# A transpose on one core: TensorE's program as a loop with decrementing semaphores, and the load issued ahead of the pending store

## Chip, cores, metric

One Trainium2 chip, one of its cores. The metric is the device time of the core in microseconds (us), the median of several executions. Input and output are 256 MB each in HBM, the memory outside the core.

## The reference

```python
def setup_inputs():
    return {"x": np.random.randn(8192, 8192).astype(np.float32)}

def reference(x):
    return np.transpose(x)
```

## The kernel before

The matrix is handled in 128 *row chunks*, in two *slabs* (column halves) of 64. A chunk is 128 rows by 4096 columns, 2 MB. It is loaded into one of three buffers in SBUF, the core's own memory. TensorE transposes it in 32 blocks of 128 x 128, four blocks to a bank of PSUM (the memory that TensorE writes), eight banks. ScalarE copies the even banks and VectorE the odd ones into *regions*; a region collects one group of four output row blocks over eight chunks (2 MB) and is then stored. Windows are staggered, so that in the steady state each chunk closes exactly one window: per chunk one 2 MB load and one 2 MB store. At the end of a slab all eight windows close at once, with 1 to 8 chunks in them (256 KB to 2 MB). All DMAs go through one queue, issued by SyncE.

```python
S, B, W = 32, 4, 8
NR, NIN, NREG, NPS = S // B, 3, 9, 8
...
for t in range(NIN):
    load(t)
n = 0
for t, (s, c) in enumerate(chunks):
    nc.tensor.wait_ge(s_ld[t % NIN], 16 * (t // NIN + 1))    # counts that only grow
    closing = []
    for q in [(c + k) % NR for k in range(NR)]:              # the order turns with the chunk
        if q not in window:
            ... r = free.pop(0); the copy engine waits until region r's last store has landed
        ps = pss[n % NPS]
        if bank[n % NPS] is not None:
            nc.tensor.wait_ge(*bank[n % NPS])
        for b in range(B):
            last = nc.tensor.transpose(ps[...], ins[t % NIN][...], ident)
        last.then_inc(s_pe, 1)
        n += 1
        (nc.scalar, nc.vector)[e].wait_ge(s_pe, n)
        cp = ... copy of the bank into the region
        cp.then_inc(s_cp[e], 1)
        copied[e] += 1
        bank[(n - 1) % NPS] = (s_cp[e], copied[e])
        if c == end:
            closing.append((q, e, copied[e]))
    for q, e, count in closing:                              # the pending store first
        nc.sync.wait_ge(s_cp[e], count)
        ... store of the region
    if t + NIN < len(chunks):                                # then the next load
        nc.sync.wait_ge(s_pe, n)
        load(t + NIN)
```

## Time and profile before

| | before |
|---|---|
| time, median of 3 | 1266.07 us (1265.91 to 1267.67) |
| DMA rate over the span | 425 GB/s; 426 to 431 in nearly all slices |
| TensorE busy | 57% |
| one row chunk (load + store) | 9.79 us in the mean |
| median 16 KB DMA packet | 611 ns, so 16 engines move 429 GB/s |

First the slices of the profiled execution (the span in 40 equal parts: busy tenths of the DMA engines, then GB/s), with the DMA queues below (packets, MB, share of the 16 engines' span):

```profile
DMA  9999999999999999999999999999999999999998
GB/s 380 418 428 427 428 429 428 427 428 428 426 428 429 426 428 430 429 428 428 428 417 428 428 427 428 431 429 429 429 428 428 430 428 430 429 429 429 428 428 353
DMA packets 39308, 537.51 MB, mean 425 GB/s; under 512 B 4320, under 2 KB 4832, under 8 KB 6240
## 3 DMA queue, kind: packets, MB, share of 16 engines
q1 hardware_dynamic: 39264, 536.89, 100.0%
q8 instruction: 32, 0.52, 0.2%
q14 instruction: 12, 0.10, 0.0%
```

The kernel is bound by its DMA engines from end to end: no slice but the first two (380 and 418), the slab change (417) and the last is more than 1% off the 429 GB/s that the packets allow. Besides the data, 32 packets of 16 KB carry instructions (q8). They come about every 39 us (the median), which is four chunks, so one per 256 of TensorE's 8192 matrix instructions; one takes 1.0 us at the median (0.94 to 1.10). I call them *fetches*. (q14 is a second queue of instruction packets, 12 of 8 KB, 309 ns each.)

Then the waits (engine and line, for whom; us in total, times, longest):

```profile
ACT reg L142 <- PE ps L131: 902.7, 501, 7.7
DVE reg L144 <- PE ps L131: 850.8, 499, 10.3
PEld ps L131 <- DMA in<-in_x_dram: 520.8, 123, 6.1
...
ACT reg L142 <- DMA out_dram<-reg: 33.8, 6, 13.5
DVE reg L144 <- DMA out_dram<-reg: 33.4, 5, 18.1
```

Everybody waits down a chain that starts at the load. The copies wait for a store only 11 times, and 65 of these 67 us are at the slab change: in the steady state a region is free just in time.

The DMA issues (KB each, median us from issue to landing):

```profile
in<-in_x_dram SPq DMA_DIRECT2D x128, 2048.0 KB, 23.5
out_dram<-reg SPq DMA_DIRECT2D x114, 2048.0 KB, 22.7
```

23.5 us is almost five transfers of 4.9 us: the queue is always deep.

One more reading needs the trace itself. The trace has 16 increments of a semaphore for each transfer, each with its own time (4320 for the 270 transfers), and the profile counts 16 DMA engines. I read them as one from each engine, when its share has landed; the pace agrees (at 16 packets of 611 ns an engine needs 9.78 us per chunk, and loads 75 to 127 landed 9.79 us apart in the mean), but the trace does not say which engine an increment belongs to. Read so, the 16 times, here sorted, show how far the engines have come apart. The times of three transfers, in us after the first of the 16:

```
load 0           0.0 .. 0.3                                                            spread 0.3
load 20          0.0 .. 2.8                                                            spread 2.8
last store       0.0 0.1 0.1 0.5 0.7 1.0 1.8 2.6 3.3 4.2 4.4 4.7 5.5 5.5 5.9 5.9       first at 1257.7 us, last at 1263.7
```

The spread grows mostly in steps: five of 1.0 to 1.6 us, each seen at a load that landed 3 to 8 us after the start of an instruction packet. The kernel waits for all 16 increments of its stores, so it ends with the slowest of the 16 engines (1263.7 us, in a span of 1265.1).

### The profile page before, as it was taken

The page shows a single profiled execution, that of the slowest core. Times are in us where ns is not written, and L with a number is a line of the kernel's source. Part 1 is how long each engine was busy: PE and PEld are TensorE (multiplying, and loading weights), DVE is VectorE, ACT ScalarE, POOL GpSimd, SP SyncE. Part 2 cuts the span into 40 slices and gives each one's busy share as a digit, 9 for nine tenths or more (in the row PEclk, how much of TensorE's full clock was granted, in tenths as well). Part 3 has the DMA queues.
Part 4 walks back from the last instruction along what each step waited for, and adds up shares of the span by engine and source line. Part 5 has one row for each costly group of instructions (what it writes and reads, how often), then busy time and mean ns, then how long its engine had stood idle before and what let it go on. Part 6 is the DMA issues. An engine that isn't in the chain of part 4 may idle for free.

```text
span 1265.1 us, 9814 instructions
## 1 busy us (share of the span) xinstructions
PE 722.6 (57%) x4096; PEld 690.6 (55%) x4096; DVE 353.5 (28%) x512; ACT 300.7 (24%) x513; POOL 0.7 (0%) x6
## 2 busy tenths in 40 slices
PE   6555656665556555565456655656566555665651
PEld 6555645555456555564455555655455555565551
DVE  3322222322223222232133322223223222232220
ACT  3322222222222222222122222222222222222220
POOL 0000000000000000000000000000000000000000
PEclk8877686777776877768667777686867877777675
DMA  9999999999999999999999999999999999999998
GB/s 380 418 428 427 428 429 428 427 428 428 426 428 429 426 428 430 429 428 428 428 417 428 428 427 428 431 429 429 429 428 428 430 428 430 429 429 429 428 428 353
DMA packets 39308, 537.51 MB, mean 425 GB/s; under 512 B 4320, under 2 KB 4832, under 8 KB 6240
## 3 DMA queue, kind: packets, MB, share of 16 engines
q1 hardware_dynamic: 39264, 536.89, 100.0%
q8 instruction: 32, 0.52, 0.2%
q14 instruction: 12, 0.10, 0.0%
HBM read 268.44 MB, written 268.44 MB: 424 GB/s over the span
## 4 chain that ended last, share of the span: by engine, by line
DMA 78%; PE 20%; issue 0%; DVE 0%; ACT 0%; SPq 0%; ACTq 0%
DMA in<-in_x_dram 75%; PE ps L131 20%; DMA out_dram<-reg 2%; DVE reg L144 0%; ACT reg L142 0%; SPq L197 0%; SPq L68 0%; ACTq L140 0%
## 5 line engine op out<-in xcount | busy, mean ns | idle before, releaser
L131 PE MATMUL ps<-ident,in 128*128 128x128 f32 x4096 | 722.6, 359 | 514.8 <-DMA in<-in_x_dram 499.7
L131 PEld LDWEIGHTS ps<-ident,in 128*128 128x128 f32 x4096 | 690.6, 193 | 546.5 <-DMA in<-in_x_dram 520.8
L144 DVE COPY reg<-ps 128x512 f32<-128x512 f32 x512 | 353.5, 692 | 884.2 <-PE ps L131 850.8
L142 ACT COPY reg<-ps 128x512 f32<-128x512 f32 x512 | 299.4, 586 | 936.5 <-PE ps L131 902.7
L142 ACT ACT_TABLE_LOAD x1 | 1.3, 1283 | 0.9 <-SPq L68 0.9
L83 POOL TENSOR_SCALAR_AFFINE_SELECT ident<-ident 128x128 f32<-128x128 f32 x1 | 0.3, 292 | 0.2 <-POOL ident L81 0.2
L81 POOL MEMSET ident<- 128x128 f32 x1 | 0.2, 204 | 0.5 <-SPq L68 0.5
L186 POOL MEMSET const-bfloat16-1.0<- 128x1 bf16 x1 | 0.1, 101 | 0.0
L186 POOL MEMSET const-uint8-127<- 128x1 uint8 x1 | 0.1, 101 | 0.0
L186 POOL MEMSET const-float32-0.0<- 128x1 f32 x1 | 0.1, 98 | 0.2 <-issue 0.2
L186 POOL MEMSET const-float32-1.0<- 128x1 f32 x1 | 0.1, 98 | 0.0
## 6 DMA issues: line engine op xcount, KB each, us to landing
in<-in_x_dram SPq DMA_DIRECT2D x128, 2048.0 KB, 23.5
out_dram<-reg SPq DMA_DIRECT2D x114, 2048.0 KB, 22.7
out_dram<-reg SPq DMA_DIRECT2D x4, 1792.0 KB, 20.1
out_dram<-reg SPq DMA_DIRECT2D x4, 1536.0 KB, 19.2
out_dram<-reg SPq DMA_DIRECT2D x4, 1280.0 KB, 19.1
out_dram<-reg SPq DMA_DIRECT2D x4, 1024.0 KB, 17.9
out_dram<-reg SPq DMA_DIRECT2D x4, 768.0 KB, 16.3
out_dram<-reg SPq DMA_DIRECT2D x4, 512.0 KB, 13.2
```

The costliest lines, as they stand in the source:

```text
L81: nc.gpsimd.memset(ident, 0.0).then_inc(s_id, 1)
L83: nc.gpsimd.affine_select(out=ident, in_=ident, compare_op=mybir.AluOpType.not_equal, fill=1.0, base=0, pattern=[[-1, P]], channel_multipl ...
L131: last = nc.tensor.transpose(ps[:, b * P:(b + 1) * P], ins[t % NIN][:, (q * B + b) * P:(q * B + b + 1) * P], ident,)
L142: cp = nc.scalar.copy(out=o, in_=i)
L144: cp = nc.vector.tensor_copy(out=o, in_=i)
L186: nc = _bacc.Bacc("TRN2", target_bir_lowering=False, num_devices=1)
```

## The change

The intent: TensorE's 8192 matrix instructions become two chunks written out and 42 turns of a loop over three chunks, so that the fetches all along the run fall away. Every turn of this loop runs the same instructions, with the same counts and the same banks: so the counts do not grow, but each semaphore is brought down when it has been waited for, and each bank has its own; and the bank order does not turn with the chunk, but is fixed. And SyncE issues the next load ahead of the pending store.

```diff
-        pss = [... for k in range(NPS)]
+        pss = [... for k in range(NR)]
+        s_bank = [nc.alloc_semaphore(f"s_bank{q}") for q in range(NR)]
+        def transposes(t):
+            k = t % NIN
+            nc.tensor.sem_inc(s_ld[k], -16).wait_op(s_ld[k], 16, "sem-ge")
+            for q in range(NR):
+                if t:
+                    nc.tensor.sem_inc(s_bank[q], -1).wait_op(s_bank[q], 1, "sem-ge")
+                for b in range(B):
+                    tr = nc.tensor.transpose(pss[q][...], ins[k][...], ident)
+                    if b == B - 1:
+                        tr.then_inc(s_pe, 1)
+        for t in range(T % NIN):
+            transposes(t)
+        with nc.Fori(0, T // NIN, engines=[nc.tensor.engine]):
+            for t in range(NIN):
+                transposes(T % NIN + t)
...
-            nc.tensor.wait_ge(s_ld[t % NIN], 16 * (t // NIN + 1))
-            for q in [(c + k) % NR for k in range(NR)]:
+            for q in range(NR):
...
-                cp.then_inc(s_cp[e], 1)
-                copied[e] += 1
-                bank[(n - 1) % NPS] = (s_cp[e], copied[e])
                 if c == end:
+                    cp.then_inc(s_cp[e], 1)
+                    copied[e] += 1
                     closing.append((q, e, copied[e]))
+                    eng.wait_ge(s_cp[e], copied[e])
+                    eng.sem_inc(s_bank[q], 1)
+                else:
+                    cp.then_inc(s_bank[q], 1)
+            if t + NIN < T:
+                nc.sync.wait_ge(s_pe, (t + 1) * NR)
+                load(t + NIN)
             for q, e, count in closing:
                 ... store
-            if t + NIN < len(chunks):
-                nc.sync.wait_ge(s_pe, n)
-                load(t + NIN)
```

More of the change, by code (lines that the diff above doesn't have):

```diff
@@ L63 @@
     NREG = 9
-    NPS = 8
     CH = N // P
@@ L72 @@
         regs = [nc.alloc_sbuf_tensor(f"reg{k}", [P, B * W * P], dt).ap() for k in range(NREG)]
-        pss = [nc.alloc_psum_tensor(f"ps{k}", [P, B * P], dt).ap() for k in range(NPS)]
+        pss = [nc.alloc_psum_tensor(f"ps{k}", [P, B * P], dt).ap() for k in range(NR)]
         s_id = nc.alloc_semaphore("s_id")
@@ L91 @@
         ).then_inc(s_id, 1)
-        nc.tensor.wait_ge(s_id, 2)
         chunks = [(s, c) for s in range(M // J) for c in range(CH)]
@@ L100, in load @@
             ).then_inc(s_ld[t % NIN], 16)
+        def transposes(t):
[5 more added lines that the diff above has]
+                for b in range(B):
+                    tr = nc.tensor.transpose(
+                        pss[q][:, b * P:(b + 1) * P],
+                        ins[k][:, (q * B + b) * P:(q * B + b + 1) * P],
+                        ident,
+                    )
+                    if b == B - 1:
+                        tr.then_inc(s_pe, 1)
+        T = len(chunks)
+        nc.tensor.wait_ge(s_id, 2)
+        for t in range(T % NIN):
[3 more added lines that the diff above has]
+                transposes(T % NIN + t)
         for t in range(NIN):
             load(t)
-        n = 0
         copied = [0, 0]
-        bank = [None] * NPS
         free = list(range(NREG))
@@ L112 @@
         for t, (s, c) in enumerate(chunks):
-            nc.tensor.wait_ge(s_ld[t % NIN], 16 * (t // NIN + 1))
             closing = []
-            for q in [(c + k) % NR for k in range(NR)]:
+            for q in range(NR):
+                e = q % 2
+                eng = (nc.scalar, nc.vector)[e]
                 if q not in window:
@@ L121 @@
                     if stored[r]:
-                        (nc.scalar, nc.vector)[q % 2].wait_ge(s_st[r], 16 * stored[r])
+                        eng.wait_ge(s_st[r], 16 * stored[r])
                 c0, end, r = window[q]
@@ L125 @@
                 view = regs[r][:, :B * rows].rearrange("p (b i) -> p b i", b=B)
-                ps = pss[n % NPS]
-                e = q % 2
-                if bank[n % NPS] is not None:
-                    nc.tensor.wait_ge(*bank[n % NPS])
-                for b in range(B):
-                    last = nc.tensor.transpose(
-                        ps[:, b * P:(b + 1) * P],
-                        ins[t % NIN][:, (q * B + b) * P:(q * B + b + 1) * P],
-                        ident,
-                    )
-                last.then_inc(s_pe, 1)
-                n += 1
                 o = view[:, :, (c - c0) * P:(c - c0 + 1) * P]
-                i = ps.rearrange("p (b i) -> p b i", b=B)
-                (nc.scalar, nc.vector)[e].wait_ge(s_pe, n)
+                i = pss[q].rearrange("p (b i) -> p b i", b=B)
+                eng.wait_ge(s_pe, t * NR + q + 1)
                 if e == 0:
```

## The prediction

> **What bounds it now.** The DMA engines. The slices show them over 90% busy, at 426 to 431 GB/s nearly everywhere; the queue table gives 537.5 MB in 1265.1 us. TensorE is busy 57%. A row chunk takes 9.87 us (two 2 MB transfers), its 32 transposes 4 to 6 us (timeline). DMA is 78% of the chain of waits. A 16 KB packet takes 611 ns at the median: 429 GB/s for 16 engines, the bytes' own limit.
>
> Not all of the span is bytes. The last slice has 353 GB/s. The 16 increments of the last store land from 1257.7 to 1263.7 us: the slowest engine ends 5.9 us after the fastest, and the kernel waits for it. This spread is 0.3 us at the start and steps up by about 1.5 us when one of the 32 instruction packets of q8 (16 KB, about 1.0 us each) falls on an engine that was not ahead. They come every 39 us, which is four chunks, 256 TensorE instructions. [...] 32 x 1.5 us over 16 engines is 3 us in the mean, about 6 us on the slowest.
>
> **What the change does.**
> 1. TensorE's 8192 instructions become two chunks plus a loop of three (about 220 instructions, 14 KB). If the loop stays resident, q8 falls from 32 packets to 2 to 5. The slowest engine then ends near the fastest's time less its own fetches: 0.5 us under 1257.7, plus 1 to 1.5 us of skew from the small q14 fetches, which stay. Gain about 5 us.
> 2. About 9 decrements per chunk on TensorE. At 51 ns each in this trace: 0.5 us per chunk, off the path.
> 3. Fixed bank order and load before store. The load is issued no earlier (it still waits for the chunk's last transpose); the store goes out about 5 us later, one queue place (4.9 us) behind. It lands some 10 us later against the loads. A region that was free just in time (store landed 322.7 us, wanted at about 323) now holds up copies until about 15 us after their chunk landed, and so TensorE's next chunk. By my recurrence the next load is still issued 13 us before its place in the queue begins, so the engines should not run dry. New waits, no time lost.
>
> **Time.** 1266.07 - 5 = about 1261 us; range 1257 to 1272. Faster by 2% would need under 1241, which 537 MB at 429 GB/s (1251 us) excludes. Faster 1%, same 95%, slower 4%.
>
> **What would show it.** q8 at 5 packets or fewer; last landings within 2 us; last slice near 390 GB/s; copies waiting for store DMAs in most chunks (over 300 us, not 67); load to landing 20, not 23.5 us.
>
> **What would make it wrong.** [...] Slower by 2% needs the queue to run dry: GB/s below 425 in every slice.

The sum came to 1266.07 - 5 = about 1261 us: 5.9 us of spread that the last stores show, less the 1 to 1.5 us for q14, plus 0.5, make the 5. The q14 figure is an estimate of mine, the 14 KB of the loop is 220 times the 64 bytes that 32 packets of 16 KB come to over 8192 instructions, and that the loop stays resident was an assumption. On a loop that fetches at every turn, with one chance in three, the prediction named 1268 to 1278 us.

## The result

| | before | changed |
|---|---|---|
| median of 4 runs | 1266.87 us (1265.91 to 1269.5) | 1269.79 us (1268.77 to 1272.34) |
| ratio | | 1.0023, 95% interval 1.0001 to 1.0045: the same, within 2% |
| span of the profiled run | 1265.1 us | 1267.8 us |

A ratio is the mean time of one kernel's fast runs over that of the other's of the same rounds, so not quite the ratio of the medians. The time lies inside the predicted range, but a gain of 5 us was predicted and it became 3 us longer.

The slices and queues of the changed kernel:

```profile
DMA  9999999999999999999999999999999999999997
GB/s 384 418 428 426 430 428 430 430 428 430 429 428 430 429 429 430 429 430 430 426 380 428 428 429 430 430 430 430 430 429 430 430 430 430 428 428 430 430 429 315
DMA packets 39277, 537.00 MB, mean 424 GB/s; under 512 B 4320, under 2 KB 4832, under 8 KB 6240
## 3 DMA queue, kind: packets, MB, share of 16 engines
q1 hardware_dynamic: 39264, 536.89, 99.8%
q14 instruction: 12, 0.10, 0.0%
q8 instruction: 1, 0.02, 0.0%
```

The instruction packets went from 32 to 1, and most slices are a little faster (430 where there was 428). But the slab change fell from 417 to 380 and the last slice from 353 to 315.

Its waits and issues:

```profile
ACT reg L154 <- DMA out_dram<-reg: 780.1, 66, 17.3
DVE reg L156 <- DMA out_dram<-reg: 770.5, 66, 23.9
PEld ps L111 <- issue: 598.0, 201, 9.3
PE ps L111 <- PEq L109: 541.9, 187, 9.1
```

```profile
in<-in_x_dram SPq DMA_DIRECT2D x128, 2048.0 KB, 19.6
out_dram<-reg SPq DMA_DIRECT2D x114, 2048.0 KB, 24.4
```

The copies now wait for stores about once per chunk (132 times), 1551 us in all, as predicted, and the loads sit shorter in the queue. TensorE's waits stand under its sequencer (PEq) now; the trace has 1147 semaphore instructions on TensorE, 51 ns each, where the kernel before has 131. None of this starves the engines in the steady state: 430 GB/s.

Where the time went is seen in the landings. I split each run at four transfers, and give the slowest and the mean of the 16 engines. In the changed kernel the load stands one place (4.89 us, eight packets of 611 ns) earlier in the queue than before, so 4.89 is added to its first stretch and taken from its last:

| us | to load 60 | loads 60 to 75 (slab change) | loads 75 to 127 | to the end | sum |
|---|---|---|---|---|---|
| slowest, before | 573.9 | 148.3 | 509.2 | 32.2 | 1263.7 |
| slowest, changed | 573.5 | 149.7 | 511.0 | 32.3 | 1266.5 |
| mean, before | 571.4 | 148.0 | 509.0 | 32.2 | 1260.6 |
| mean, changed | 569.6 | 150.6 | 507.9 | 33.9 | 1262.1 |

The mean engine gains 1.8 us in the first slab and 1.1 us in the second, the 3 us of fetches that were predicted. It gives back 2.6 us at the slab change and 1.7 us at the end. And the slowest engine, which sets the time, gains almost nothing in the first slab (0.4 us) and *loses* 1.4 us at the slab change and 1.7 us (before rounding) in the second slab: these make the 2.8 us. At the last load the 16 increments stand like this (us after the first):

```
before    0.0 0.1 0.1 0.5 0.6 1.0 1.9 2.6 3.2 4.2 4.4 4.7 5.4 5.5 5.9 5.9
changed   0.0 0.0 0.1 0.1 0.2 0.5 0.5 0.9 1.2 1.3 1.3 1.4 1.7 2.2 4.4 7.4
```

Before, with the fetches, the engines are spread over 5.9 us, none more than 1.0 us behind the next. Now fourteen engines lie within 2.2 us, and one is 7.4 us behind. In the second slab its lag over the first engine grows by 68 ns per chunk (the median over loads 75 to 126), nearly every chunk. Before, this median is 0: there the lag mainly jumps, by 1.35 and 1.46 us, at loads that landed at 677 and 987 us, 4 and 7 us after the start of a fetch. I call this steady growth the *drift*. With it comes a set of 16 KB packets of 625 to 640 ns, slightly too long, which fall mostly in times when TensorE transposes (83% of them at their middle, against 56% of all 16 KB packets): 196 in the changed kernel, 40 in the one before (between 80 and 1200 us, without 600 to 700). That they run on the engine that falls behind is not shown; their time over 611 ns sums to 3.9 us (0.8 before), less than that engine's lag.

### The profile page after: what moved, and what is told of

The parts are those of the page before. It is cut to its first block, busy times and chain, and to the rows that moved or that the text cites. A ratio compares the mean times of both kernels' runs of the same rounds, so it can differ in the third digit from the quotient of the medians.

```text
span 1267.8 us, 11057 instructions
## 1 busy us (share of the span) xinstructions
PE 685.6 (54%) x4096; PEld 637.6 (50%) x4096; DVE 330.2 (26%) x512; ACT 278.2 (22%) x513; POOL 0.7 (0%) x6
## 5 line engine op out<-in xcount | busy, mean ns | idle before, releaser
L111 PE MATMUL ps<-ident,in 128*128 128x128 f32 x4096 | 685.6, 342 | 551.0 <-PEq L109 541.9
L111 PEld LDWEIGHTS ps<-ident,in 128*128 128x128 f32 x4096 | 637.6, 182 | 598.8 <-issue 598.0
L156 DVE COPY reg<-ps 128x512 f32<-128x512 f32 x512 | 330.2, 686 | 908.5 <-DMA out_dram<-reg 770.5
L154 ACT COPY reg<-ps 128x512 f32<-128x512 f32 x512 | 276.9, 597 | 960.7 <-DMA out_dram<-reg 780.1
## 6 DMA issues: line engine op xcount, KB each, us to landing
in<-in_x_dram SPq DMA_DIRECT2D x128, 2048.0 KB, 19.6
out_dram<-reg SPq DMA_DIRECT2D x4, 1536.0 KB, 19.6
out_dram<-reg SPq DMA_DIRECT2D x4, 512.0 KB, 15.1
```

Source lines behind the costliest of these rows:

```text
L111: tr = nc.tensor.transpose(pss[q][:, b * P:(b + 1) * P], ins[k][:, (q * B + b) * P:(q * B + b + 1) * P], ident,)
L154: cp = nc.scalar.copy(out=o, in_=i)
L156: cp = nc.vector.tensor_copy(out=o, in_=i)
```

## The experiments

Eighteen runs, each beside runs of the kernel before on the same chip. "Drift" and "packets" are as just defined, from the one profile of each run. "Last load" is the lag of the last engine there.

| run | median us | ratio, 95% interval | q8 packets | drift, ns per chunk | packets | last load, us |
|---|---|---|---|---|---|---|
| before | 1266.87 | | 32 | 0 | 40 | 5.9 |
| changed | 1269.79 | 1.0023 (1.0001 to 1.0045) | 1 | 68 | 196 | 7.4 |
| e1_unrolled | 1267.82 | 1.0005 (0.9988 to 1.0021) | 36 | 44 | 243 | 5.5 |
| e2_store_first | 1268.7 | 1.0012 (0.9986 to 1.0039) | 1 | 101 | 440 | 10.5 |
| e3_big_first | 1269.23 | 1.0016 (1.0000 to 1.0031) | 1 | 66 | 207 | 6.2 |
| e4_before_load_first | 1268.53 | 1.0006 (0.9990 to 1.0022) | 32 | 1 | 74 | 6.1 |
| e5_before_fixed_order | 1267.22 | 1.0002 (0.9986 to 1.0017) | 32 | 8 | 40 | 5.8 |
| e6_before_decrements | 1267.78 | 1.0000 (0.9985 to 1.0016) | 36 | 93 | 399 | 9.0 |
| e7_more_semaphores | 1274.45 | 1.0056 (1.0040 to 1.0072) | 1 | 103 | 222 | 10.1 |
| e8_few_semaphores | 1270.33 | 1.0026 (1.0011 to 1.0041) | 1 | 59 | 194 | 6.4 |
| e9_decrement_loads | 1266.0 | 0.9991 (0.9974 to 1.0008) | 32 | 1 | 36 | 6.3 |
| e10_decrement_banks | 1268.56 | 1.0022 (0.9995 to 1.0048) | 35 | 0 | 32 | 6.2 |
| e11_idle_semaphores | 1271.91 | 1.0041 (1.0019 to 1.0062) | 36 | 0 | 86 | 6.2 |
| e12_closing_step | 1266.39 | 0.9992 (0.9974 to 1.0010) | 32 | 0 | 35 | 6.3 |
| c1_changed_again | 1269.69 (one) | | 1 | 66 | 189 | 9.3 |
| c2_decrements_again | 1270.67 (one) | | 36 | 96 | 433 | 9.5 |
| c3_banks_again | 1268.7 (one) | | 35 | 2 | 60 | 6.3 |
| c4_idle_sems_again | 1267.57 (one) | | 36 | 0 | 155 | 6.2 |
| f1_loads_on_act | 1268.2 | 1.0003 (0.9985 to 1.0020) | 1 | 80 | 182 | 9.5 |
| f2_loads_on_act_orders | 1273.43 | 1.0031 (1.0005 to 1.0058) | 1 | 101 | 480 | 10.6 |

The kernel before, run beside them, itself scatters from 1265.2 to 1271.5 us, with 11 of its 40 runs in the timed batches above 1269. So a difference of 1 or 2 us in time is not settled by six runs; the landings in the profiles tell more than the times, but each is of one run.

The drift is a median: it tells whether the lag grows steadily, not by how much. It parts the kernels clearly in the second slab: with it the lag grows by over 20 ns in 61 to 100% of the chunks, without it in 8 to 20%. In the mean the growth is 66 ns per chunk in the changed kernel and 33 in the one before, but 57 in e1 (drift) and 58 in c4 (none). In the first slab (loads 10 to 60) the median is 0 to 102 ns in the kernels with drift and -16 to 0 in the others; an engine that falls behind shows in this measure only once it is the last.

### e1: without the loop

```diff
-        for t in range(T % NIN):
+        for t in range(T):
             transposes(t)
-        with nc.Fori(0, T // NIN, engines=[nc.tensor.engine]):
-            for t in range(NIN):
-                transposes(T % NIN + t)
```

> The changed kernel with TensorE's loop written out, decrements and order kept. Theory F (the loop saves the instruction fetches): q8 rises from 1 packet to 32 or more, each costs one engine 1.5 us, so about 3 us per engine in the mean and 1 to 3 us in time: 1271 to 1273 us, ratio to the kernel before 1.003 to 1.005. Rival L (the loop itself costs, by a slow drift of one DMA engine, 60 ns per chunk, that the kernel before does not show): the last engine no longer drifts, and the time is 1266 to 1269 us.

Measured: 1267.8 us. The queues of this kernel:

```profile
q1 hardware_dynamic: 39264, 536.89, 100.0%
q8 instruction: 36, 0.59, 0.2%
q14 instruction: 12, 0.10, 0.0%
```

The fetches are back, 36 of them, and the mean pace of the engines in the second slab is 9.797 us per chunk instead of 9.768. That is the cost of the fetches, 29 ns per chunk, as the first theory says. But the kernel is not slower for it, as far as the runs tell (ratio 1.0005 against 1.0023, with intervals that overlap). So the saved fetches are real and do not show in the time. The rival half fell too: the drift is there (44 ns) without the loop. It does not belong to the loop.

### e2: the store issued first again

```diff
-            if t + NIN < T:
-                nc.sync.wait_ge(s_pe, (t + 1) * NR)
-                load(t + NIN)
             for q, e, count in closing:
                 ... store
+            if t + NIN < T:
+                nc.sync.wait_ge(s_pe, (t + 1) * NR)
+                load(t + NIN)
```

> The changed kernel with the store issued before the load again; loop, decrements and fixed bank order kept. Theory R (putting the load ahead delays the register regions, and the waits of the copies cost the time): copies' waits for store DMAs fall from 1550 us to under 300 us and the time falls by 3 us or more, to 1263 to 1266 us. Rival O (the order of the eight closing stores at the end of a slab costs it): the waits fall all the same, but the time stays within 1.5 us of 1269.8, since the 2 MB store still comes last.

Its waits:

```profile
ACT reg L154 <- PE ps L111: 737.9, 388, 9.8
DVE reg L156 <- PE ps L111: 708.1, 389, 10.4
...
ACT reg L154 <- DMA out_dram<-reg: 209.4, 47, 12.2
DVE reg L156 <- DMA out_dram<-reg: 186.6, 40, 16.5
```

The waits for stores fell from 1551 us to 396 us, somewhat less than expected, and the time is 1268.7 us, not 1263 to 1266. Waits of that size off the critical path were worth nothing that the runs can show; theory R has no support. One of its six runs took 1265.35 us and another 1275.61.

### e3: the oldest window stored first at a slab's end

With the fixed order the 2 MB store came last, behind the 256 KB one. In the changed kernel's trace SyncE's issue of each of the last five stores ended when four earlier transfers had still to land in full, 0.5 to 1.7 us after the fifth before it had landed on its last engine, and with small transfers ahead four are little work. (Of the 13 issues at the two slab ends that took over 0.8 us, 10 ended with four transfers, of 256 KB to 2 MB, still to land, the others with five or six; before the change 11 of 13.) So the 2 MB store's issue ended at 1255.7 us, when the first engines had finished everything ahead of it (the store before it landed on its first engine at 1254.5).

```diff
+            closing.sort(key=lambda k: window[k[0]][0])
             for q, e, count in closing:
```

> The changed kernel, but at the end of each slab the eight stores are issued oldest window first (the 2 MB one, then 1792 KB down to 256 KB), as in the kernel before. Theory O: no engine runs dry at 1254 to 1256 us, the middle loses nothing, and the time falls by 3 to 5 us, to 1265 to 1267 us; last slices near 350 GB/s and 415 GB/s instead of 315 and 380. Rivals R and L: the time stays at 1269 to 1270 us.

Measured: 1269.2 us. The slices:

```profile
GB/s 386 418 429 428 428 429 430 430 429 429 430 429 428 430 430 430 429 429 429 428 376 425 429 430 429 429 429 430 430 430 429 430 428 429 429 429 430 429 428 328
```

376 and 328 against 380 and 315: the slab change is no better and the end only a little. The mean engine still takes 38.7 us from the last load to the end, as in the changed kernel (38.8). But this is no clean test of the order. With the fixed order the oldest window belongs to bank 7, which is copied last, so the store that is now the first of the eight had to wait for the end of VectorE's copies (1233.17 + 4.39 = 1237.56 us):

```profile
1233.17 4.39 DVE L156 COPY reg<-ps 128x512 f32<-128x512 f32 x6 [11.30 <-DMA out_dram<-reg]
1237.59 2.58 SPq L28 DMA_DIRECT2D out_dram<-reg  x3
```

That is 9.5 us after the last load had landed (2.0 us in the changed kernel), and the first engine landed this 2 MB store 7.5 us after the one ahead of it, instead of 4.9: the fast engines ran dry there instead. Two other readings settle theory O as far as the time goes. The slowest engine takes 32.2 to 32.4 us from the last load to the end in all 20 profiles (with 4.89 taken off where the load goes ahead), whatever the order. And e5 below, which stores in the same order as the changed kernel but has no drift, takes on the slowest engine 148.4 us for the slab change, where the kernel before takes 148.3.

### e4 and e5: one part of the change in the kernel before

e4 moves the load ahead of the pending store in the kernel before, as the last lines of the change do; e5 fixes the bank order there:

```diff
-            for q in [(c + k) % NR for k in range(NR)]:
+            for q in range(NR):
```

> The kernel before with nothing changed but the load issued ahead of the pending store. Theory R: register waits appear in most chunks and the time rises by 2 to 4 us, ratio 1.002 to 1.003. Theory O: register waits appear, but the queue does not run dry and the stores keep their falling order, so the ratio is 0.999 to 1.001.

> The kernel before with the banks in fixed order 0 to 7, nothing else. Theory D (one DMA engine is slowed a little in every chunk by what TensorE's decrementing semaphore instructions do; seen as 16 KB packets of 625 to 640 ns, 40 to 75 in the kernels without decrements, 200 to 440 in those with): under 100 such packets, no steady drift of the last engine between the fetch steps, time 1266 to 1268 us. Rival X (the fixed order brings the drift): 200 or more such packets and a drift of 50 to 100 ns per chunk.

Measured: ratios 1.0006 and 1.0002, no drift in either (1 and 8 ns). e4 has the region waits (508 us on ScalarE, 482 us on VectorE) and is not slower within the error. Neither part alone costs anything that can be shown, and neither brings the drift. Rival X fell.

### e6: the decrements alone

The kernel before with its turning order and no loop, but with the changed kernel's semaphores:

```diff
-            nc.tensor.wait_ge(s_ld[t % NIN], 16 * (t // NIN + 1))
+            nc.tensor.sem_inc(s_ld[t % NIN], -16).wait_op(s_ld[t % NIN], 16, "sem-ge")
...
-                    nc.tensor.wait_ge(*bank[n % NPS])
+                    nc.tensor.sem_inc(s_bank[n % NPS], -1).wait_op(s_bank[n % NPS], 1, "sem-ge")
... and the copies count s_bank up, as in the change
```

> The kernel before, unrolled and with its turning bank order, but with TensorE waiting and decrementing as the changed kernel does (9 semaphore instructions per chunk). Theory D: 200 or more packets of 625 to 640 ns, a drift of the last engine of 50 to 100 ns per chunk, time 1267 to 1270 us. Rival X: under 100 such packets, no drift, time as before within 1 us.

Measured: 399 packets, 93 ns per chunk, 9.0 us of lag at the last load: the drift is there. The time is 1267.8 us, and the profiled run was the slowest of its five (1269.81). So the drift comes with the semaphores that are brought down; it needs neither the loop nor the fixed order nor the load ahead.

### e7 and e8: more and fewer semaphore instructions

```diff
e7:                 nc.tensor.sem_inc(s_bank[q], -1).wait_op(s_bank[q], 1, "sem-ge")
+                    nc.tensor.sem_inc(s_dum, 1)
+                    nc.tensor.sem_inc(s_dum, -1)
e8, before the eight banks of a chunk, with one s_bank for all:
+            if t:
+                nc.tensor.sem_inc(s_bank, -NR).wait_op(s_bank, NR, "sem-ge")
```

> The changed kernel with 16 more semaphore instructions per chunk on TensorE (up one, down one, of no use): 25 instead of 9. Theory D: the drift of the last engine grows from about 65 to 120 ns per chunk or more, and the time to 1273 us or more. Rival X: drift and time stay as in the changed kernel, 1268 to 1270 us.

> The changed kernel with one bank semaphore that TensorE brings down by eight once per chunk: 2 semaphore instructions per chunk instead of 9. Theory D: drift under 30 ns per chunk, under 100 packets of 625 to 640 ns, the last engine ends 3 us or more earlier: 1264 to 1267 us. Rival X: drift stays near 65 ns per chunk and the time at 1268 to 1270 us. If TensorE's waiting for all eight copies made the queue run dry instead, the GB/s would fall below 425 in all slices and the time go over 1275 us.

e7: 103 ns, and 1274.5 us, the largest loss of all runs. The drift grew by half while the instructions nearly tripled. e8: 59 ns with two instructions per chunk instead of nine, 1270.3 us. So the drift does not go with the number of semaphore instructions; theory D, as I had put it, fell in e8.

### e9 to e12: the decrements taken apart

In the kernel before: e9 has only the first of e6's two edits, e10 only the second. e11 keeps the growing counts and adds nine semaphore instructions per chunk that nobody waits for. e12 adds only the copy engines' extra step:

```diff
e11:                nc.tensor.sem_inc(s_dum, 1)          # for each bank; and sem_inc(s_dum, -NR) per chunk
                    nc.tensor.wait_ge(*bank[n % NPS])
e12:            if c == end:
                    closing.append((q, e, copied[e]))
+                   eng.wait_ge(s_cp[e], copied[e])
+                   eng.sem_inc(s_dum[e], 1)
```

> The kernel before, where TensorE brings down only the load semaphores (by 16, once per chunk); banks as before. If the semaphore that the DMA engines count up is what matters (theory D-load): about 400 packets of 625 to 640 ns and a drift of the last engine near 90 ns per chunk, as in the run with all decrements (399 packets, 93 ns). Rivals: under 100 packets, no drift. Time within 2 us of before either way.

> The kernel before, where TensorE brings down only the bank semaphores (8 times per chunk, and the copy engines' extra step for a closing window); loads as before. If it is semaphore instructions on TensorE as such (theory D-count) or the banks' (theory D-bank): 200 or more packets of 625 to 640 ns, drift 50 to 100 ns per chunk. Theory D-load: under 100 packets, no drift.

> The kernel before with 9 semaphore instructions per chunk on TensorE that nobody waits for (8 up by one, one down by eight). Theory D-count: 200 or more packets of 625 to 640 ns and a drift of 50 to 100 ns per chunk. If what matters is that TensorE waits in a semaphore instruction (theory D-wait), or theory D-load or D-bank: under 100 packets, no drift.

> The kernel before, where only the copy engines do the changed kernel's extra step after a window's last copy (wait for the copy itself, then count a semaphore up, here one that nobody reads). If that step brings the drift (theory C): 200 or more packets of 625 to 640 ns and a drift over 50 ns per chunk. All other theories: under 100 packets, no drift, time as before within 1 us.

Measured: no drift in any, although e9 and e10 together make e6. But all four ran on a chip on which no drifting kernel stood beside them, so this alone proves little. And e11 took 1271.9 us, ratio 1.0041, without any drift in its profile; that profile is of the fastest of its four runs (1267.02; the others 1271.5 to 1273.3). What its slower runs did, no trace shows.

### c1 to c4: the same, with controls on one chip

c1 is the changed kernel again and c2 is e6 again, as controls; c3 is e10 and c4 is e11. One run each; the kernel before, beside them, took 1270.22 us in its one run, so these times say nothing.

> The changed kernel again, as a control on this chip. If the drift belongs to the kernel: 150 or more packets of 625 to 640 ns and about 65 ns of drift per chunk. If it belongs to the chip or to chance: under 100 packets, no drift, and the last engine ends 3 us or more earlier than 1266.5.

> The kernel before with all decrements again (399 packets and 93 ns per chunk on chip 14), as a second control. Drift belongs to the kernel: 200 or more packets, 50 to 100 ns per chunk. Chip or chance: under 100 packets, no drift.

> Decrements of the banks alone, beside the controls. With drifting controls: if the banks' decrements suffice, 200 or more packets and 50 ns per chunk or more; if both kinds of decrement are needed (as the runs on chip 6 would say), under 100 packets and no drift.

> Nine semaphore instructions per chunk that nobody waits for, beside the controls. With drifting controls: if semaphore instructions on TensorE as such suffice, 200 or more packets and 50 ns per chunk or more; if not, under 100 packets and no drift.

Measured: 66 and 96 ns in the controls, 2 and 0 in the others. The drift is the kernel's, on this third chip as on the two before. Neither the banks' decrements alone nor semaphore instructions as such bring it. (In c4 there are 155 long packets without drift, so the packets are the weaker sign of the two.)

### f1 and f2: the load semaphore brought down by ScalarE

TensorE waits for the load semaphore without touching it; ScalarE brings it down before it copies bank 0, which TensorE must see freed before it can come to that buffer again.

```diff
-            nc.tensor.sem_inc(s_ld[k], -16).wait_op(s_ld[k], 16, "sem-ge")
+            nc.tensor.wait_ge(s_ld[k], 16)
...
                 eng.wait_ge(s_pe, t * NR + q + 1)
+                if q == 0:
+                    eng.sem_inc(s_ld[t % NIN], -16)
```

f2 adds the edits of e2 and e3.

> The changed kernel, but the load semaphore is brought down by ScalarE (before it copies bank 0), not by TensorE, which only waits. If TensorE's decrement of the load semaphores makes the drift and the drift eats the gain: under 100 packets of 625 to 640 ns, drift under 20 ns per chunk, lag of the last engine under 4 us at the last load, its end 1260 to 1263.5 us in the trace, time 1263 to 1267 us, ratio 0.997 to 1.000. If any decrement of the load semaphores makes it, or the drift belongs to the loop: 60 ns per chunk again and 1268 to 1271 us.

> As the run before, with the store issued before the load and the oldest window stored first at the end of a slab. If the order effects at the slab ends matter once the drift is gone: 1 to 3 us less than the run before, 1262 to 1265 us, ratio 0.996 to 0.999. If not: the same within 1 us.

Measured: 80 and 101 ns; 1268.2 and 1273.4 us. So it is not TensorE's decrement of the load semaphore. The profiled runs were slow ones of their sets (f1 1272.87, its others 1267.2 to 1269.6; one of f2's runs took 1265.15). f2's order has the flaw of e3: the first of its last eight stores was issued 6.7 us after the last load had landed, and landed on its first engine 11 us after the one ahead of it. No version beat the kernel before beyond the error.

## Why the prediction was wrong

**Right.** The bound (the DMA engines), and that both kernels stay in the neighbourhood of 1260 to 1270 us (1266.87 and 1269.79). q8 fell to 1 packet, at 24.0 us, in the loop's first turn. The one chance in three of a fetch at each turn did not come true: 42 turns of 221 instructions, after 138 written out, and no further packet. That the time nevertheless lies within the 1268 to 1278 us named for that case is chance. The fetches' cost was right: 3 us predicted for the mean engine, 1.8 + 1.1 us measured in the two slabs; for 16 engines and the 27 fetches that fell away there it is 1.7 us each. (No wait of TensorE stands under them in the kernel before: its matrix instructions waited 499.7 us for loads and 15.1 us for copies.) The new region waits came in size and without starving the queue, and load to landing was 19.6 us (20 predicted).

**The step that failed** is "The slowest engine then ends near the fastest's time less its own fetches: 0.5 us under 1257.7, plus 1 to 1.5 us of skew from the small q14 fetches, which stay. Gain about 5 us." It took the fetches for the only thing that sets one engine back. In the changed kernel the last store landed on its first engine at 1261.6 us, where about 1257.2 was predicted, and on its last 4.8 us later, where 1 to 1.5 was predicted. The runs showed what else sets engines back:

- In all 11 profiles of kernels in which both the load and the bank semaphores are brought down (the changed kernel twice, e1, e2, e3, e6 twice, e7, e8, f1, f2) one engine drifts by 44 to 103 ns per chunk. In the 9 profiles without (before, e4, e5, e9, e10 twice, e11 twice, e12) the drift is 0 to 8 ns. For loads 75 to 127 the slowest engine needs 510.9 to 516.4 us in the 11 and 508.9 to 510.5 us in the 9. In the changed kernel its lag grew by 3.4 us over these 52 chunks, against 1.7 us before, and was 7.4 us at the last load, against the 5.9 us that the fetches had left. So the gain of the other engines had no worth: the last increment came at 1266.5 us instead of 1263.7, and the increments of the last eight stores were 4.8 to 7.5 us apart, not "within 2 us".
- The second item of the prediction weighed the decrements only on TensorE ("off the path"); there a semaphore instruction did take 51 ns, and the loop's branch 208 ns at the median. That was the place to look, though not for TensorE's time.
- "Slower by 2% needs the queue to run dry" was not put to the test (no run was slower by 2%), but at the slab change and at the end the fast engines do lose: 2.6 and 1.7 us in the mean. The last slice was predicted "near 390 GB/s" and was 315. These do not set the time at the end, where the slowest engine loses only 0.1 us. The fast engines' loss there goes with the issues: the issue of each of the last five stores ended 0.5 to 1.7 us after the fifth transfer before it had landed on the slowest engine too (0.7 to 1.8 us before the change), and in the changed kernel the 2 MB store is the last of them, with little work ahead of it. At the slab change the slowest engine loses 1.4 us as well, half of the 2.8 us; which part of the change brings that is not shown (e4, with the load ahead and no drift, takes 150.2 us there on its slowest engine, but e1, with the load ahead and drift, 147.8). A part of the mean engine's loss is packets that took long. Over 611 ns, the 16 KB packets between 640 and 672 us lost 7 engine-us in the kernel before and 45 in the changed one; divided by 16 engines that is 2.4 us, about the loss. Both the load ahead and the loop seem to bring it: 3 to 20 in the kernels with neither, 22 and 27 with the load ahead only (e1, e4), 22 and 25 with the loop only (e2, f2), 36 to 45 with both. Why is not known.

**Theories that fell:** that the late 2 MB store costs the time (e5 and the slowest engine's end, not e3), that the region waits do (e2, e4), that the loop itself does (e1), that the fixed order brings the drift (e5), that the drift goes with the number of semaphore instructions (e8), that TensorE's decrement of the load semaphore is the cause (f1).

**Open.** By what way semaphores that are brought down would slow one DMA engine is not shown, nor which engine it is. That both kinds are needed is only partly shown: the banks alone were tried beside drifting controls (c3), the loads alone (e9) only on a chip without a control. Why e10 and e11 had runs of 1271 to 1274 us is open too: their profiles are of fast runs. In e10 and c3 2.6 to 2.8 us of the time lie outside the profiled span, 1.8 to 1.9 in the others, so some 0.8 us of theirs is nothing that the trace shows. And since the profiles are one run each, the drift's share in the times is an inference: e6 drifts as much as any and its median is only 1 us over that of the kernel before; and e11 took 1271.5 us or more in three of four runs, while its one profile, of the fourth, has no drift.

## What to carry to other kernels

Here the DMA engines bound, and the kernels ended with the slowest of the 16 (at 1263.7 and 1266.5 us, in spans of 1265.1 and 1267.8). In such a kernel ask of a saving whether it reaches *that* engine, and read the 16 increments of a late transfer before pricing it: a mean of 3 us was saved here and the time did not fall. Do not put an instruction off the account because its own engine has time to spare; here what came with the semaphores showed up in the DMA landings, as one engine that fell behind by 44 to 103 ns per chunk in 11 of 11 profiles. And when an experiment shows nothing, check that a kernel which is known to show the effect does so on the same chip.
